# Queueing VectorE's attention side work behind the minima, moving late stores to GpSimd, and loading a branch's gates earlier

## The chip, the cores and the metric

The kernel runs on one core of a Trainium2 chip. The metric is device time in microseconds, the median of several executions. One further execution was recorded by the hardware profiler, and all rows below come from it.

## The reference

One hybrid decoder layer over 1024 tokens of width 1024, in float32:

```
h    = RMSNorm_pre(x)
proj = h @ w_in -> z_ssm | xBC | dt | q | k | v | f | z_att | g_ssm | g_att
A    = Mamba-2 chunked scan of conv+silu(xBC), gated by silu(z_ssm), group norm
B    = causal attention, 16 heads of 64:
       softmax(q.k/8 + F[t] - F[s]) @ v * silu(z_att),  F = cumsum(log_sigmoid(f))
m    = sigmoid(g_ssm) * (A @ w_branch_ssm) + sigmoid(g_att) * (B @ w_branch_att)
out  = x + RMSNorm_post(m @ w_out)
```

A is the recurrence branch ("ssm"), B the attention branch.

## The kernel before, in words

**Products in steps.** All large products run through a class `Stream`. It takes pairs of 128-column units and computes each 2 x 2 block product in seven steps (numbered 1 to 7) in place of eight, from sums of weight blocks and differences of data blocks. A step is 12 matmuls of 128 x 512; float32 operands are split into a high part (ScalarE copies into float32r) and a low part (VectorE subtracts). Split weights are called `wop` (L349, L350), split data operands `x0h`, `x0l` to `x6h`, `x6l` (L275 to L279). `Stream.half()` emits half a step. At a step's start it also calls `prepare`, which sums and splits the weights of the step three later, and `Operands.some`, which fetches and splits data operands of the next product that builds up. What a product is used for stands in handlers: `dst` gives the place of a result block, `post` works on it (tanh gates, silu gates, the gated branch results), and `begin` loads what `post` will need.

**The stages.** First normalisation and transposes; then the projections run beside the recurrence (generators `ssd` and `gate_and_norm`), one of four groups after another; then attention, with the remaining projections (the gates "za", "gs", "ga") and the product A @ w_branch_ssm ("wbs", handler `gated`) and the start of B @ w_branch_att ("wba") as filling between its parts; then the rest of "wba" and the product with w_out.

**Attention.** 8 pairs of heads with 6 visits each, 48 visits `m`. A visit does, in program order: `scores` (two query blocks for two heads, four score tiles `s`; VectorE adds the bias and takes the row minimum in one operation, L1471; ScalarE takes the exponential, L1475), the weighted sums of the visit before (`av`), `free` (VectorE scales the sums, L1423), `deferred` work (differences of attention outputs), `stream.release()`, some halves of the stream ("ahead"), `turned` (transposes `pt` of the exponentials, copied to SBUF as `p`, by VectorE at L1512 in blocks with b % 4 == 1 of the first six pairs of heads and by ScalarE at L1514 elsewhere), `stream.hold()`, and more halves ("behind"). Between `hold` and `release` the calls of `Operands.some` are collected, and `release` makes them after the next visit's scores; `prepare` is called at once.

**What sets the order.** TensorE's instructions stay in program order (`keep_in_program_order`). On the other engines a scheduler orders instructions ahead of the run by simulated readiness and priority; `tc.high_priority()` raises some, `pin` keeps an instruction behind the one traced before it on its engine, and `tc.issue_after(x)` keeps what is traced inside it behind x on x's engine, in issue order only. Once built, each engine and each queue of DMA issues runs strictly in order. SyncE (SP) issues nearly all loads; stores go through SP, ScalarE's queue (ACT) and GpSimd's (POOL).

**Small tiles.** `small()` gives one of four rotating 128 x 512 tiles (tag "th"), shared by gates, loads and results.

Of the kernel before, what the change touches and what calls it, by code (L numbers as in the profile page):

```python
# [23 lines left out]
NG = 4  # L24
# [62 lines left out]
def hybrid_layer(ctx: ExitStack, tc, a, out):  # L87

    nc = tc.nc
# [230 lines left out]
    class Pair:  # L320
# [95 lines left out]
                    nc.vector.tensor_tensor(d, s, ps, ALU.subtract)  # L416
            post(ch)

        def do(self, which):
            if which in (2, 4, 3) or which in (5, 7) and self.sums:  # L420
                unit, ch = {2: (0, 0), 4: (1, 0), 3: (0, 1)}.get(which, (1, 1))
                for begin in self.handlers[unit][2:]:
                    begin(ch)
            if which == 1:
                pool, tag = self.bank
                self.b = pool.tile([P, HALF], F32, tag=tag, bufs=1, name="pb")
                yield from self.matmuls(self.b, 1, "b11", True)
                self.k1 = self.keep(self.b)
            elif which == 2:
                pool, tag = self.other  # L430
                ps = pool.tile([P, HALF], F32, tag=tag, bufs=1, name="p" + tag)
                yield from self.matmuls(ps, 2, "b21", True)
                self.give(0, 0, ps, self.k1, "sum")
            elif which == 6:
                yield from self.matmuls(self.b, 6, "-t2", False)
                self.k2 = self.keep(self.b)
            elif which in (5, 7):
                if which == 5:
                    self.c = pj.tile([P, HALF], F32, tag="c", bufs=1, name="pc")
                    yield from self.matmuls(self.c, 5, "t1", True)  # L440
                else:
                    yield from self.matmuls(self.b, 7, "t3", False)
                    self.k7 = self.keep(self.b)
                self.sums += 1
                if self.sums == 2:
                    self.give(1, 1, self.c, self.k7, "less")
            elif which == 4:
                yield from self.matmuls(self.b, 4, "t4", False)
                self.give(1, 0, self.b)
            elif which == 3:  # L450
                yield from self.matmuls(self.c, 3, "-b22", False)
                self.give(0, 1, self.c, self.k2, "from")

    class Stream:
# [6 lines left out]
        def __init__(self, pairs, double, last):  # L461
            self.pairs = pairs
            for n, p in enumerate(pairs):
                p.bank, p.other = (pj, "be"[n % 2]), (pjx, "d") if n < double else (pj, "c")

                p.between = n < double or n >= last

            p, q, r = pairs[0:3]
            self.steps = [(p, 1), (q, 1), (p, 2), (q, 2)] + [(p, n) for n in (6, 5, 7, 4, 3)]
            self.steps += [(q, 6), (q, 5), (q, 7), (r, 1), (q, 4), (q, 3)]  # L470
            for n in range(2, last):
                p, nxt = pairs[n], pairs[n + 1]
                self.steps += [(p, i) for i in ((2, 6, 5, 7) if n < double else (6, 2, 7, 5))] + [(nxt, 1)]
                self.steps += [(p, 4), (p, 3)] if n + 1 < last else [(p, 3), (p, 4)]

            a, b, c, d, e, f, g, h = pairs[last:]
            self.steps += [(a, 5), (a, 6), (a, 7), (b, 1), (a, 2), (a, 4), (a, 3)]
            for p, nxt in ((b, c), (c, d), (d, e)):
                self.steps += [(p, 2), (p, 6), (p, 5), (p, 7), (nxt, 1), (p, 4), (p, 3)]
            self.steps += [(f, 1), (e, 2), (e, 6), (e, 5), (e, 7), (f, 2), (e, 4), (e, 3)]  # L480
            self.steps += [(f, 6), (f, 5), (f, 7), (g, 1), (f, 4), (f, 3)]
            self.steps += [(g, 2), (g, 6), (g, 5), (g, 7), (h, 1), (g, 4), (g, 3)]
            self.steps += [(h, 6), (h, 5), (h, 7), (h, 2), (h, 3), (h, 4)]
            self.following = {p: n.ops for p, n in zip(pairs, pairs[1:]) if n.ops is not p.ops}
            self.building = []
            self.chores, self.line = [], []
            self.held = None
            self.count = 0
            self.at = 0
            self.run = None  # L490
            self.waiting = []
            self.loads = [(p, names) for p in pairs for names in (("a11", "a12"), ("a21", "a22"))]
            self.loaded = []
            self.load_next()
# [23 lines left out]
                self.prepare(p, which)  # L518

        def prepare(self, p, which):  # L520
            p.prepare(which)
            self.load_more()

        def after(self, halves, fn):

# [2 lines left out]
        def half(self):  # L528
            if self.run is None:
                if self.at == len(self.steps):  # L530
                    return False
                p, which = self.steps[self.at]
                if which == 7 and p.ops is ops_a and "merged" not in fin:
                    return False
                if p.ops is ops_a and not all(p.ops.ready(OPERAND[which].strip("-"), j) for j in range(KH)):
                    return False
                self.ahead(False)
                for ops in self.building:
                    ops.some(OPERAND[which])
                self.run = p.do(which)  # L540
                next(self.run)
            else:
                for _ in self.run:
                    pass
                self.run = None
                p, which = self.steps[self.at]
                if p in self.following:
                    ops = self.following[p]
                    if ops not in self.building:
                        self.building.append(ops)  # L550
                    ops.open(OPERAND[which])
                self.ahead(True)
                self.at += 1
            for ops in self.building:
                if self.held is None:
                    ops.some()
                else:
                    self.held.append(ops)
            for chores in (self.chores, self.line):
                if chores:  # L560
                    chore = chores.pop(0)
# [13 lines left out]

        def release(self):
            held, self.held = self.held or [], None
            for ops in held:
                ops.some()

        def do_chores(self):
            while self.chores:
# [24 lines left out]
                self.halves(n)  # L607


    def tanh_gate(dram, i):  # L610

        t = {}

        def dst(ch):
            t[ch] = small()
            return t[ch]

        def post(ch):
            nc.scalar.activation(t[ch], t[ch], AF.Tanh, scale=0.5)
            nc.scalar.dma_start(dram[i, :, half(ch)], t[ch])  # L620

        return dst, post

    def silu_gate(dram, i):

        t = {}

# [4 lines left out]
        def post(ch):  # L632
            th = small()
            nc.scalar.activation(th, t[ch], AF.Tanh, scale=0.5)
            nc.vector.scalar_tensor_tensor(th, th, 1.0, t[ch], ALU.add, ALU.mult)
            nc.sync.dma_start(dram[i, :, half(ch)], th)

        return dst, post

# [335 lines left out]
    def gate_and_norm(g):  # L975
# [23 lines left out]
        for ch in range(2):  # L999
            sl = half(ch)  # L1000
            for j in range(2):
# [3 lines left out]
                        xs[j][:, sl], xs[j][:, sl], ng[:, i : i + 1], r[ch], ALU.mult, ALU.mult  # L1005
                    )
                )
                nc.sync.dma_start(ys_dram[i, :, sl], xs[j][:, sl])
                yield 1

    def weights_work():
# [23 lines left out]
    order = [p for ps in by_group for p in ps]  # L1035

    order[0:4] = [both("gs", 0, lambda i: tanh_gate(gs_dram, i))] + [order[n] for n in (2, 1, 3, 0)]
    late = [both("za", g, lambda i: silu_gate(za_dram, i)) for g in range(4)]
    late += [both("gs", g, lambda i: tanh_gate(gs_dram, i)) for g in range(1, 4)]
    late += [both("ga", g, lambda i: tanh_gate(ga_dram, i)) for g in range(4)]  # L1040


    fin = {}

    def gated(i):

        t = {}

        def begin(ch):
            t[ch] = small(), small()  # L1050
            nc.sync.dma_start(t[ch][1], gs_dram[i, :, half(ch)])

        def dst(ch):
            return t[ch][0]

        def post(ch):
            stream.after(1, lambda: times(*t[ch], ch))

        def times(y, g, ch):
            nc.vector.scalar_tensor_tensor(y, g, 1.0, y, ALU.add, ALU.mult)  # L1060
# [232 lines left out]
    with tc.tile_pool(name="att", bufs=1, reuse_waits="tile", side="right") as ap, tc.tile_pool(  # L1293
# [148 lines left out]
        def scores(hp, g, u):  # L1442
# [23 lines left out]
            for e in range(2):  # L1466
                o = ex[:, e, u, 0:w]
                nm = hd.at(hd.nm, i, h, e)
                with tc.high_priority():
                    pin(  # L1470
                        nc.vector.tensor_tensor_reduce(  # L1471
                            o, s[e][:, 0:w], fb[hp, h][:, e, 0:w], 1.0, 3.0e38, ALU.add, ALU.min, nm
                        )
                    )
                    pin(nc.scalar.activation(o, o, AF.Exp, scale=-1.0, bias=nm, accum_out=hd.at(hd.sm, i, h, e)))  # L1475

        def turned(hp, g, sent):

# [16 lines left out]
            for b in order:  # L1495
# [13 lines left out]
                with tc.high_priority():  # L1509

                    if b % 4 == 1 and hp < NK - 2:
                        nc.vector.tensor_copy(to, src)  # L1512
                    else:
                        nc.scalar.activation(to, src, AF.Copy)  # L1514
                made[b] = (hp, g, b, first, p)
# [135 lines left out]
        for m in range(6 * NK + 1):  # L1651
# [6 lines left out]
                    scores(hp, g, u)  # L1658
            for one in made:
                weighted(*one)  # L1660
            for hd, which in end(m - 1):
                hd.free(which)
            if m == 6 * NK:
                stream.release()
                heads[NK - 1].out(2)
                break
            for hd, which in end(m - 2):
                if hd.last and which and m < 6 * NK - 1:
                    hd.out(which)
            for fn in deferred:  # L1670
                fn()
            deferred.clear()
            stream.release()
            for hd, which in end(m):
# [84 lines left out]
```

## Time and profile before

| | us |
|---|---|
| median of 3 runs | 1279.64 |
| lowest, highest | 1279.46, 1281.26 |
| profiled execution | 1278.67 |
| its span, first to last instruction | 1277.0 |

The granted clock of TensorE was 0.998 of full speed. Attention's first scores start at 684.5 us and its last minima are past 1113 us. The profile gives, for each engine, busy time and the idle time before instructions with what ended it; PEld is TensorE's weight load, whose starts show when TensorE really began a matmul, since a matmul's end is modelled.

### The profile page before, as it was taken

The numbers are of one execution on the slowest core, as the hardware profiler recorded it, in microseconds if no ns is written. First come the engines' busy times: TensorE is split into PE (matmuls) and PEld (weight loads), VectorE is DVE, ScalarE is ACT, GpSimd is POOL, SyncE is SP. The second block draws the span as 40 slices with busy tenths as digits, with TensorE's granted clock in tenths as the row PEclk, the third lists the DMA queues.
The fourth block names the chain that finished last, engine by engine and source line by source line (L and its number), as shares of the span: only waits on it lengthen the run. The fifth ranks groups of instructions, "written<-read, shape, count | busy, mean of one in ns | idle before, by whom it ended". The sixth has DMA issues, their size and how long they took to land.

```text
span 1277.0 us, 20793 instructions
## 1 busy us (share of the span) xinstructions
PE 1246.0 (98%) x6926; PEld 980.9 (77%) x6926; DVE 1009.9 (79%) x1994; ACT 795.1 (62%) x1738; POOL 312.4 (24%) x314
## 2 busy tenths in 40 slices
PE   5999999999999999999999999999999999999997
PEld 3688888788788888888877777777767777778886
DVE  7988896888888978997766667767789767886975
ACT  7745665556665765566555666666677666744754
POOL 4000440013400241114102123313111212366052
PEclk9999999999999999999999999999999999999999
DMA  8233452546336533644447566666687657766932
GB/s 296 71 120 75 144 168 87 186 149 191 122 113 214 174 125 115 220 152 133 141 153 255 166 225 203 213 222 215 233 291 261 216 173 251 252 214 199 362 112 102
DMA packets 152747, 233.56 MB, mean 183 GB/s; under 512 B 15200, under 2 KB 60736, under 8 KB 152640
## 3 DMA queue, kind: packets, MB, share of 16 engines
q1 hardware_dynamic: 136640, 197.13, 47.4%
q10 hardware_dynamic: 11136, 19.11, 4.0%
q0 software_dynamic: 4864, 15.99, 3.3%
q8 instruction: 54, 0.88, 0.3%
q14 instruction: 53, 0.43, 0.1%
HBM read 162.99 MB, written 72.34 MB: 184 GB/s over the span
## 4 chain that ended last, share of the span: by engine, by line
PE 75%; DVE 8%; DMA 6%; ACT 5%; issue 4%; POOL 1%; SPq 1%; DVEq 0%; ACTq 0%; POOLq 0%
PE pb L128 31%; PE pc L128 18%; PE pd L128 6%; PE av L128 4%; PE pt L131 4%; PE s L128 4%; PE yps L128 2%; DVE wop L350 1%; ACT ex L1475 1%; PE st L128 1%; DMA xt<-in_x 1%; DMA th<-ys_dram 1%; DVE ex L1471 1%; PE tr L131 1%; PE tr_v L131 1%
## 5 line engine op out<-in xcount | busy, mean ns | idle before, releaser
L349 ACT ACTIVATE wop<-sum 128x512 fp32r<-128x512 f32 x180 | 112.5, 626 | 109.7 <-DVE sum L355 52.9
L350 DVE TENSOR_TENSOR wop<-sum,wop 128x512 fp32r<-128x512 f32 x180 | 137.8, 767 | 52.0 <-ACT wop L349 51.0
L1475 ACT ACTIVATE ex<-ex,nm 128x512 f32<-128x512 f32 (+1 forms) x192 | 116.2, 606 | 74.0 <-DVE nm L1471 73.2
L402 ACT ACTIVATE s<-pb 128x512 f32<-128x512 f32 x144 | 85.3, 592 | 95.7 <-PE pb L128 94.4
L128 PE MATMUL pc<-x2h,wop 128*128 128x512 f32 x384 | 130.4, 398 | 0.6 <-DVE u L414 0.6
L128 PE MATMUL pb<-x5h,wop 128*128 128x512 f32 x384 | 130.1, 396 | 1.0 <-ACT s L402 0.9
L128 PE MATMUL pb<-x0h,wop 128*128 128x512 f32 x384 | 130.8, 397 | 0.0
L128 PE MATMUL pb<-x6h,wop 128*128 128x512 f32 x384 | 129.5, 395 | 1.3 <-ACT s L402 1.3
L128 PE MATMUL pc<-x3h,wop 128*128 128x512 f32 x384 | 129.7, 395 | 0.4 <-DVE ot L416 0.4
L128 PE MATMUL pb<-x4h,wop 128*128 128x512 f32 x384 | 129.2, 395 | 0.0
L350 DVE TENSOR_TENSOR wop<-raw,wop 128x512 fp32r<-128x512 f32 x144 | 103.8, 722 | 28.4 <-ACT wop L349 27.9
L1471 DVE CUSTOM_DVE_ANT_0 ex<-s,fb 128x512 f32<-128x512 f32 (+1 forms) x192 | 97.0, 551 | 20.5 <-PE s L128 15.4
L349 ACT ACTIVATE wop<-raw 128x512 fp32r<-128x512 f32 x144 | 89.7, 624 | 11.4 <-PE pd L128 6.3
L128 PE MATMUL pd<-x1h,wop 128*128 128x512 f32 x288 | 96.3, 394 | 0.0
L128 PEld LDWEIGHTS pb<-x5h,wop 128*128 128x128 f32 x384 | 72.1, 188 | 18.9 <-ACT s L402 2.2
L128 PEld LDWEIGHTS pb<-x6h,wop 128*128 128x128 f32 x384 | 72.1, 188 | 18.6 <-issue 2.1
L128 PEld LDWEIGHTS pc<-x2h,wop 128*128 128x128 f32 x384 | 72.1, 188 | 18.6 <-issue 2.4
L128 PEld LDWEIGHTS pb<-x0h,wop 128*128 128x128 f32 x384 | 72.1, 188 | 17.4 <-issue 2.9
L128 PEld LDWEIGHTS pc<-x3h,wop 128*128 128x128 f32 x384 | 72.1, 188 | 17.1 <-issue 1.5
L128 PEld LDWEIGHTS pb<-x4h,wop 128*128 128x128 f32 x384 | 72.1, 188 | 16.7 <-issue 1.9
L211 POOL TENSOR_TENSOR wd<-wd 128x256 f32<-128x256 f32 x32 | 31.8, 995 | 206.1 <-DMA wd<-in_wo 120.9
L131 PE MATMUL pt<-ident,ex 128*128 128x128 f32 x576 | 75.5, 273 | 3.6 <-DVE nm L1471 1.8
(311 smaller groups left out, 2986.6 us busy)
## 6 DMA issues: line engine op xcount, KB each, us to landing
raw<-in_wu SPq DMA_DIRECT2D x128, 256.0 KB, 4.6
csb<-cs_dram SPq DMA_DIRECT2D x32, 256.0 KB, 6.5
q<-q_dram SPq DMA_DIRECT2D x32, 256.0 KB, 4.2
k<-k_dram SPq DMA_DIRECT2D x16, 512.0 KB, 6.7
fb<-f_dram SPq DMA_DIRECT2D x16, 512.0 KB, 5.7
rb<-st_dram SPq DMA_DIRECT2D x48, 128.0 KB, 3.1
wd<-in_wo SPq DMA_DIRECT2D x40, 128.0 KB, 2.5
xt<-in_x SPq DMA_DIRECT2D x8, 512.0 KB, 6.7
```

Source lines behind the costliest of these rows:

```text
L128: return tc.keep_in_program_order(nc.tensor.matmul(*args, **kw))
L131: return tc.keep_in_program_order(nc.tensor.transpose(out_, in_, idn))
L211: pin(nc.gpsimd.tensor_tensor(t[out_], t[a_], t[b_], ALU.subtract))
L349: nc.scalar.activation(op[:, 0], src, AF.Copy)
L350: nc.vector.tensor_tensor(op[:, 1], src, op[:, 0], ALU.subtract)
L402: nc.scalar.activation(s, ps, AF.Copy)
L1471: nc.vector.tensor_tensor_reduce(o, s[e][:, 0:w], fb[hp, h][:, e, 0:w], 1.0, 3.0e38, ALU.add, ALU.min, nm)
L1475: pin(nc.scalar.activation(o, o, AF.Exp, scale=-1.0, bias=nm, accum_out=hd.at(hd.sm, i, h, e)))
```

## The change

Three parts.

1. *Queueing.* `Stream.front` holds the last minimum of the running visit, and after the transposes VectorE's copy, where there is one. `stream.behind()` is `tc.issue_after(front)`: weight preparation, operand splits, released work, `free` and the deferred differences are traced inside it, so that VectorE issues them behind that instruction. `prepare` is now collected between `hold` and `release` too.
2. *Stores.* The silu gates "za", the attention gates "ga" of units 6 and 7, and the recurrence's result ys of the last group are stored through GpSimd's queue, in place of SP's, ScalarE's and SP's.
3. *Gates.* In `gated`, the load of the gate from gs_dram is marked `early` and made at the start of the step before the one that needs it; the tile of the result is now taken when the result is written.

```diff
-        def do(self, which):
-            if which in (2, 4, 3) or which in (5, 7) and self.sums:
+        def begin(self, which, sums, early):
+            if which in (2, 4, 3) or which in (5, 7) and sums:
                 unit, ch = {2: (0, 0), 4: (1, 0), 3: (0, 1)}.get(which, (1, 1))
                 for begin in self.handlers[unit][2:]:
-                    begin(ch)
+                    if hasattr(begin, "early") == early:
+                        begin(ch)
+
+        def do(self, which):
+            self.begin(which, self.sums, False)
...
         def prepare(self, p, which):
-            p.prepare(which)
+            if self.held is not None:
+                self.held.append(lambda: self.prepare(p, which))
+                return
+            with self.behind():
+                p.prepare(which)
             self.load_more()
+
+        def behind(self):
+
+            return nullcontext() if self.front is None else tc.issue_after(self.front)
...
+                if self.at + 1 < len(self.steps):
+                    after, then = self.steps[self.at + 1]
+                    after.begin(then, after.sums + (after is p and which in (5, 7)), True)
                 self.run = p.do(which)
...
                 if self.held is None:
-                    ops.some()
+                    with self.behind():
+                        ops.some()
                 else:
-                    self.held.append(ops)
+                    self.held.append(ops.some)
...
             held, self.held = self.held or [], None
-            for ops in held:
-                ops.some()
+            for fn in held:
+                with self.behind():
+                    fn()
...
-    def tanh_gate(dram, i):
+    def tanh_gate(dram, i, queue=nc.scalar):
...
-            nc.scalar.dma_start(dram[i, :, half(ch)], t[ch])
+            queue.dma_start(dram[i, :, half(ch)], t[ch])
...
-    def silu_gate(dram, i):
+    def silu_gate(dram, i, queue=nc.sync):
...
-            nc.sync.dma_start(dram[i, :, half(ch)], th)
+            queue.dma_start(dram[i, :, half(ch)], th)
...
-                nc.sync.dma_start(ys_dram[i, :, sl], xs[j][:, sl])
+                queue = nc.sync if g < NG - 1 else nc.gpsimd
+                queue.dma_start(ys_dram[i, :, sl], xs[j][:, sl])
...
-    late = [both("za", g, lambda i: silu_gate(za_dram, i)) for g in range(4)]
+    late = [both("za", g, lambda i: silu_gate(za_dram, i, nc.gpsimd)) for g in range(4)]
...
-    late += [both("ga", g, lambda i: tanh_gate(ga_dram, i)) for g in range(4)]
+    late += [both("ga", g, lambda i: tanh_gate(ga_dram, i, nc.gpsimd if i >= 6 else nc.scalar)) for g in range(4)]
...
-        t = {}
+        y, g = {}, {}
 
         def begin(ch):
-            t[ch] = small(), small()
-            nc.sync.dma_start(t[ch][1], gs_dram[i, :, half(ch)])
+            g[ch] = small()
+            nc.sync.dma_start(g[ch], gs_dram[i, :, half(ch)])
+
+        begin.early = True
 
         def dst(ch):
-            return t[ch][0]
+            y[ch] = small()
+            return y[ch]
...
-                    pin(
+                    least = pin(
                         nc.vector.tensor_tensor_reduce(
...
+            stream.front = least.ins
...
                     if b % 4 == 1 and hp < NK - 2:
-                        nc.vector.tensor_copy(to, src)
+                        copy = nc.vector.tensor_copy(to, src)
+                        stream.front = copy.ins
...
-            for hd, which in end(m - 1):
-                hd.free(which)
+            with stream.behind():
+                for hd, which in end(m - 1):
+                    hd.free(which)
             if m == 6 * NK:
+                stream.front = None
                 stream.release()
...
-            for fn in deferred:
-                fn()
+            with stream.behind():
+                for fn in deferred:
+                    fn()
```

More of the change, by code (lines that the diff above doesn't have):

```diff
@@ L487, in __init__ @@
             self.held = None
+            self.front = None
             self.count = 0
@@ L1037, in hybrid_layer @@
     order[0:4] = [both("gs", 0, lambda i: tanh_gate(gs_dram, i))] + [order[n] for n in (2, 1, 3, 0)]
[L1038 removed]
+    late = [both("za", g, lambda i: silu_gate(za_dram, i, nc.gpsimd)) for g in range(4)]
     late += [both("gs", g, lambda i: tanh_gate(gs_dram, i)) for g in range(1, 4)]
[L1040 removed]
+    late += [both("ga", g, lambda i: tanh_gate(ga_dram, i, nc.gpsimd if i >= 6 else nc.scalar)) for g in range(4)]
     fin = {}
     def gated(i):
[L1047 removed]
+        y, g = {}, {}
         def begin(ch):
[L1050 to L1051 removed]
+            g[ch] = small()
+            nc.sync.dma_start(g[ch], gs_dram[i, :, half(ch)])
+        begin.early = True
         def dst(ch):
[L1054 removed]
+            y[ch] = small()
+            return y[ch]
         def post(ch):
[L1057 removed]
+            stream.after(1, lambda: times(y[ch], g[ch], ch))
         def times(y, g, ch):
```

## The prediction

> **What bounds the kernel now.** I read the page's first part, then busy time by stretches of the attention stage, then the waits of the weight loads, then the timeline at the places where they wait.
>
> ```profile
> span 1277.0 us, 20793 instructions
> PE 1246.0 (98%) x6926; PEld 980.9 (77%) x6926; DVE 1009.9 (79%) x1994; ACT 795.1 (62%) x1738; POOL 312.4 (24%) x314
> ```
>
> ```profile
> 700.00:900.00 200.00, 199.86 (x1365) 152.62 (x1364) 138.66 (x376) 131.39 (x336) 54.43 (x68) 1.00 0.63 210
> 930.00:980.00 50.00, 46.78 (x313) 34.52 (x309) 44.69 (x112) 39.59 (x98) 7.80 (x12) 1.00 0.82 280
> 1080.00:1135.00 55.00, 53.89 (x319) 40.34 (x318) 48.96 (x106) 39.77 (x94) 22.64 (x21) 1.00 0.65 222
> 1130.00:1200.00 70.00, 69.91 (x309) 57.53 (x308) 55.06 (x72) 30.26 (x54) 36.51 (x25) 1.00 0.73 245
> ```
>
> The columns are length, then busy time of TensorE, its weight loads, VectorE, ScalarE and GpSimd, clock and DMA. TensorE is full nearly everywhere at full clock, so only its holes can be won. From 700 to 900 it lacks 0.14 us; from 930 to 980, where VectorE is busy 44.69 of 50 us, it lacks 3.2. Behind attention (1130 to 1200) it is full again, so a hole closed earlier carries to the end one to one. A matmul's modelled end hides part of a hole, so I price holes by the idle time of the weight loads:
>
> ```profile
> PEld s L128 <- ACT p L1514: 7.3, 21, 0.6
> PEld pt L131 <- ACT ex L1475: 3.2, 6, 1.1
> PEld pt L131 <- DVE nm L1471: 3.0, 5, 1.1
> PEld s L128 <- DVE p L1512: 2.7, 5, 1.4
> PEld s L128 <- DVE wop L350: 1.4, 4, 0.4
> ```
>
> These are the waits between 650 and 1135 us: total, times, longest. The 7.3 us in 21 pieces of 0.35 recur whenever the stream of projections hands over to the scores, whoever is named; I take them as the price of the hand-over, which the change leaves. Left are the transposes of a visit's exponentials, which wait for ScalarE's exponential or VectorE's minimum (6.2 us together), and one wait for VectorE's copy. No projection matmul (pb, pc) waits for a split weight (wop): the 1.4 is again the hand-over to the scores.
>
> Where the holes lie:
>
> ```profile
> 952.59 0.20 PEld L131 LDWEIGHTS pt<-ident,ex 128*128 128x128 f32 x2 [0.82 <-ACT ex L1475]
> 953.89 0.14 PEld L131 LDWEIGHTS pt<-ident,ex 128*128 128x128 f32 x1 [1.10 <-DVE nm L1471]
> 956.23 0.53 PEld L131 LDWEIGHTS pt<-ident,ex 128*128 128x128 f32 x5 [1.11 <-ACT ex L1475]
> 979.29 0.54 PEld L128 LDWEIGHTS s<-k,q 64*128 64x128 f32 x5 [1.37 <-DVE p L1512]
> 1076.35 0.14 PEld L131 LDWEIGHTS pt<-ident,ex 128*128 128x128 f32 x1 [0.84 <-DVE nm L1471]
> 1076.96 0.64 PEld L131 LDWEIGHTS pt<-ident,ex 128*128 128x128 f32 x6 [0.47 <-DVE nm L1471]
> 661.82 0.19 PEld L128 LDWEIGHTS pc<-x2h,wop 128*128 128x128 f32 x1 [0.47 <-DVE th L414]
> 668.01 0.19 PEld L128 LDWEIGHTS pc<-x1h,wop 128*128 128x128 f32 x1 [0.86 <-issue]
> ```
>
> Four places: 3.03 us at 952 to 956, 1.37 at 979, 1.31 at 1076, and 1.33 ahead of attention. With the rest of the 6.2 us (6.2 - 3.03 - 1.31, about 1.9) that is some 8.9 us, the ceiling of what the change can win.
>
> **The late stores to GpSimd.** The hole at 952 starts on ScalarE:
>
> ```profile
> 945.27 0.58 ACT L1514 ACTIVATE p<-pt 128x512 f32<-128x512 f32 x1
> 948.26 0.33 ACTq L620 DMA_DIRECT2D ga_dram<-th  x1
> 948.64 1.15 ACT L278 ACTIVATE x1h<-x1l 128x512 fp32r<-128x512 f32 x2 [2.79 <-DMA fb<-f_dram]
> ```
>
> ```profile
> 949.30 1.29 DVE L279 TENSOR_TENSOR x1l<-x1l,x1h 128x512 fp32r<-128x512 f32 x2 [1.22 <-ACT x1h L278]
> 950.85 0.68 DVE L1471 CUSTOM_DVE_ANT_0 ex<-s,fb 128x512 f32<-128x512 f32 x1
> ```
>
> ScalarE ends a copy at 945.85 and then sits before its store of an attention gate until 948.26; the wait ends with the landing of another transfer (fb), not with anything the store reads. Behind it stands x1h, behind that VectorE's x1l, and behind that the visit's first minimum at 950.85. This store is one of the last pair's four (i = 6, 7), which the change sends through GpSimd's queue. There the same wait, if it comes, holds only GpSimd. I take 3.0 of the 3.03 us. [...]
>
> What the move costs on GpSimd:
>
> ```profile
> L1061 POOL DMA_DIRECT2D ms_dram<-th x16 | 8.7, 547 | 67.9 <-DVE th L1060 46.7 <-DVE ns L1388 8.7 <-DVE sm L1385 6.6
> ```
>
> 16 silu stores, 4 gate stores and the last group's 4 ys stores are 24 x 0.55 = 13 us on an engine that is 24% busy. Each now waits at GpSimd's head for its VectorE result, and the mask additions behind it feed a minimum. I take nothing, with one store's 0.55 us in front of a mask as the upper bound.
>
> The ys and silu stores leave SP's queue, where they held back loads:
>
> ```profile
> 658.60 5.50 SPq L1008 DMA_DIRECT2D ys_dram<-xs  x3
> 679.66 5.06 SPq L636 DMA_DIRECT2D za_dram<-th  x2
> ```
>
> Fourteen half steps of projections stand ahead of the first score in TensorE's order, so earlier q, k and fb loads do not start attention sooner. What can shrink is the 1.33 us at 661 and 668, where VectorE runs late after waiting for loads. Bounds 0 and 1.33; I take 0.6, the middle, since no row says which load ended it.
>
> **The queueing on VectorE.** `front` is the visit's last minimum and, where VectorE copies, then the copy. Weight preparation, operand splits, `free` and the deferred differences may not be issued ahead of it, and preparation during the second half of a visit is put off until the next visit's scores. Today such work sits between minima:
>
> ```profile
> 931.58 0.69 DVE L276 SCALAR_TENSOR_TENSOR x4l<-x4l,x4h 128x512 fp32r<-128x512 f32 x1
> 932.28 0.66 DVE L1471 CUSTOM_DVE_ANT_0 ex<-s,fb 128x512 f32<-128x512 f32 x1
> ```
>
> ```profile
> ACT ex L1475 <- DVE nm L1471: 73.2, 58, 3.2
> ```
>
> Each inserted split delays all later exponentials of the visit by 0.69 us. The 73.2 us that ScalarE waits is mostly hidden, because projections run between scores and transposes; what reaches TensorE is the 1.9 us outside the named places. Work traced in the previous visit may still slip in, so I take a third, 0.6 (bounds 0 and 1.9). At 979 the copy is the last of a VectorE run:
>
> ```profile
> 976.42 0.69 DVE L350 TENSOR_TENSOR wop<-raw,wop 128x512 fp32r<-128x512 f32 x1
> 978.82 0.41 DVE L1512 COPY p<-pt 128x256 f32<-128x256 f32 x1
> ```
>
> If that split was prepared in the visit's second half, it goes behind the copy: 0.69 of 1.37 us. I take 0.7; the x2l splits around it were traced earlier and stay.
>
> What is late next? A split put off by about half a visit:
>
> ```profile
> 979.16 0.68 DVE L1471 CUSTOM_DVE_ANT_0 ex<-s,fb 128x512 f32<-128x512 f32 x1
> ...
> 942.73 1.29 DVE L276 SCALAR_TENSOR_TENSOR x4l<-x4l,x4h 128x512 fp32r<-128x512 f32 x2
> 963.22 0.39 PE L128 MATMUL pb<-x4h,wop 128*128 128x512 f32 x1
> ```
>
> This first minimum comes three visits after that of 950.85, so a visit takes 9.4 us and half of one 5. The last x4l ends at 944.0 and its first matmul starts at 963.2, so 19 us cover that 5. I price it at nothing; with the cover gone each visit's first split would hold TensorE for up to those 5 us.
>
> **The gates of the recurrence branch.** The load of gs moves to the start of the step before, 12 matmuls and what attention puts between them sooner, and ahead of the fetches that follow.
>
> ```profile
> 1064.75 0.81 SPq L263 DMA_DIRECT2D x0l<-ya_dram  x2
> 1066.14 0.38 SPq L1051 DMA_DIRECT2D th<-gs_dram  x1
> ```
>
> ```profile
> 1071.97 0.69 DVE L1060 SCALAR_TENSOR_TENSOR th<-th 128x512 f32<-128x512 f32 x1 [4.87 <-DMA th<-gs_dram]
> ```
>
> The load stood behind an operand fetch that SP could issue only at 1064.75, and VectorE stood 4.87 us with the next visit's minima behind it: that is the hole at 1076. A load one step sooner lands before it is wanted. I take 1.3 of 1.31. Its cost: the load takes a slot of the four shared 256 KB tiles earlier, and SP waits for the slot with q, k and v behind it.
>
> **Sum.** Won: 3.0 + 0.6 + 0.6 + 0.7 + 1.3 = 6.2 us. Against it I set 1.9 us for one new chance wait of the kind at 948 (3.0 us when it strikes; with every queue reordered I count it at about two thirds). That is an estimate from one event, with bounds 0 and two events, 6.0. Net -4.3. The profiled execution took 1278.67 us (span 1277.0 and 1.67 around it), and the median of the runs, 1279.64, lies 0.97 above: 1279.64 - 4.3 = 1275.3. If everything goes and nothing comes: 1270.7.
>
> **Rivals.** A measurement of this kernel can tell about 0.2%, 2.6 us, from no change.
>
> [...]
>
> *VectorE runs out of room (slower).*
>
> ```profile
> DVE ex L1471 <- PE s L128: 15.4, 18, 1.8
> ```
>
> Today VectorE fills the time before the scores and waits for them 18 times, 0.86 us each, in 48 visits. Queued strictly, it may wait in all of them. From 930 to 980 there are five visits and 5.3 us of room: from 1.06 us more idle per visit on, VectorE sets the pace. At the longest wait seen, 1.8 us, the stretch needs 44.69 + 9.0 = 53.7 us, and 1080 to 1135 (six visits, 48.96 + 10.8) needs 59.8: 3.7 + 4.8 = 8.5 us lost. Set against the gains outside these stretches (0.6 + 0.6 + 1.3 = 2.5), that is +6.0: 1285.6. For it: 89% busy in both. Against: operands there have 19 us of slack, so a backlog can spill into the next stretch.
>
> **Chances.** Forecast 0.60, the wait that moves 0.22, VectorE out of room 0.14, and 0.04 for a slot wait on SP that costs as much. From the same cases: faster 0.60, same 0.22, slower 0.18. The range goes from 1271.0 (nearly the ceiling) to 1281.8, which holds the second case and the mild part of the third; its far part, near 1285.6, is left out.
>
> **What would show it.** Right: the 952 hole gone and no ScalarE wait of over 2 us before x1h; the four minima of a visit without splits between them and ScalarE's 73.2 us clearly lower; VectorE's wait for gs (4.87) gone; the 979 hole at about 0.7. Wrong: new waits of pb or pc for wop or an x operand; VectorE's waits for the scores growing beyond 15.4 us by over 1 us a visit from 930 to 980; SP waiting before gs with q or k behind it; or TensorE as full as forecast and the time unchanged, which would say that the holes were not the price.

## The result, and the profile after

The changed kernel takes 1283.06 us (median of 22 runs) where the kernel before took 1279.42 on the same chip (22 runs). The medians lie 3.6 us apart; the ratio of the two kernels, which leaves out one run of each that took over 2000 us, is 1.0021, with a 95% interval of 1.0012 to 1.0030. That is slower by about 2.7 us, where the forecast was 1275.3 us, faster by 4.3. The profiled execution took 1283.68 us, with a span of 1282.0 against 1277.0. Ratios below are given in the same way, and a thousandth is 1.3 us.

The page's first part, of after:

```profile
span 1282.0 us, 20839 instructions
PE 1251.5 (98%) x6926; PEld 987.2 (77%) x6926; DVE 1015.7 (79%) x1994; ACT 795.3 (62%) x1738; POOL 327.5 (26%) x338
```

TensorE loads the same weights in the same order as before. Of the 5.0 us by which the profiled span is longer, 1.7 had come up by 600 us, as far as which every engine's order is that of before (VectorE's first 876 instructions are the same, one after the other, in both traces): that much differs between single executions (in the profiles of all the kernels below it lies between -1.9 and +1.7), and is not counted below. What the change did lies between 700 and 1135 us. The busy time by stretches of after (columns as in the prediction, the clock third from the right):

```profile
700.00:900.00 200.00, 199.38 (x1357) 151.90 (x1356) 140.04 (x379) 129.34 (x331) 57.07 (x68) 1.00 0.62 204
930.00:980.00 50.00, 48.80 (x322) 36.87 (x320) 46.48 (x114) 41.95 (x102) 10.02 (x14) 1.00 0.91 303
...
1080.00:1135.00 55.00, 52.45 (x307) 39.04 (x308) 49.26 (x109) 41.76 (x99) 15.90 (x18) 0.97 0.67 226
```

From 930 to 980 TensorE now lacks 1.2 us in place of 3.2: the hole at 952 is gone. But from 700 to 900, where 0.14 us was lacking, it lacks 0.62, and the end of attention is worse (2.55 us lacking in place of 1.11, with the mean clock down to 0.97). The holes themselves, in the timeline of after's weight loads (in brackets the idle time ahead of the row and what ended it):

```profile
721.29 0.47 PEld L128 LDWEIGHTS s<-k,q 64*128 64x128 f32 x6 [0.68 <-DVE p L1535]
...
797.50 0.18 PEld L128 LDWEIGHTS s<-k,q 64*128 64x128 f32 x1 [0.57 <-ACT p L1538]
...
877.25 1.16 PEld L128 LDWEIGHTS s<-k,q 64*128 64x128 f32 x11 [0.54 <-DVE p L1535]
...
980.65 0.53 PEld L128 LDWEIGHTS s<-k,q 64*128 64x128 f32 x5 [2.14 <-DVE p L1535]
...
1078.78 0.64 PEld L131 LDWEIGHTS pt<-ident,ex 128*128 128x128 f32 x6 [0.46 <-DVE nm L1493]
1079.90 0.74 PEld L131 LDWEIGHTS pt<-ident,ex 128*128 128x128 f32 x7 [0.49 <-ACT ex L1497]
1083.83 0.18 PEld L128 LDWEIGHTS s<-k,q 64*128 64x128 f32 x1 [0.62 <-ACT p L1538]
...
1113.55 0.18 PEld L128 LDWEIGHTS s<-k,q 64*128 64x128 f32 x1 [1.43 <-ACT p L1538]
```

The waits have changed their kind. Before, the longest were those of the transposes `pt` for minima and exponentials; now they are those of the scores `s` of the next visit for the copies `p` of this one, by VectorE (721, 877 and 980) or by ScalarE (797, 1083 and 1113). The minima did get what the change is built for, and the groups of the page and of the busy time by line show who pays (after):

```profile
L1497 ACT ACTIVATE ex<-ex,nm 128x512 f32<-128x512 f32 (+1 forms) x192 | 115.9, 605 | 59.0 <-DVE nm L1493 58.9
L1493 DVE CUSTOM_DVE_ANT_0 ex<-s,fb 128x512 f32<-128x512 f32 (+1 forms) x192 | 95.6, 553 | 38.1 <-PE s L128 31.6
L1535 DVE COPY p<-pt 128x512 f32<-128x512 f32 (+1 forms) x36 | 21.5, 598 | 18.9 <-PE pt L131 13.0 <-ACT st L1419 6.0
```

and the last of these groups in the kernel before:

```profile
L1512 DVE COPY p<-pt 128x512 f32<-128x512 f32 (+1 forms) x36 | 21.5, 597 | 8.3 <-PE pt L131 7.6 <-ACT st L1397 0.6
```

ScalarE waits 58.9 us for minima in place of 73.2. But VectorE stands 31.6 us waiting for scores in place of 15.4, and 13.0 us waiting for transposes in place of 7.6, each time with the queued work behind it. It has as much to do as before, and in all it stands no longer than before: from 700 to 1135 us it is busy 327.6 us in place of 327.2, and from 650 to 1135 its waits for ScalarE's half of a split weight fall from 31.2 to 15.5 us. So the waits have moved to places ahead of minima and copies, and work has moved from there into the stretch between a visit's last minimum and its copy. The visit before 980 shows this (VectorE's timeline of after, from the last minimum to the copy):

```profile
972.76 0.28 DVE L1493 CUSTOM_DVE_ANT_0 ex<-s,fb 128x128 f32<-128x128 f32 x1
972.97 0.08 DVE L1493 DVE_READ_ACCUMULATOR2_ANT nm<- 128x1 f32 x1
972.97 0.69 DVE L350 TENSOR_TENSOR wop<-raw,wop 128x512 fp32r<-128x512 f32 x1
973.57 1.28 DVE L276 SCALAR_TENSOR_TENSOR x2l<-x2l,x2h 128x512 fp32r<-128x512 f32 x2
974.78 0.68 DVE L1445 TENSOR_TENSOR o<-av,zr 128x512 f32<-128x512 f32 x1
975.38 0.68 DVE L1599 TENSOR_TENSOR x<-x,zr 128x512 f32<-128x512 f32 x1
975.98 0.68 DVE L279 TENSOR_TENSOR x6l<-x6l,x6h 128x512 fp32r<-128x512 f32 x1
976.58 0.68 DVE L412 TENSOR_TENSOR th<-pc,s 128x512 f32<-128x512 f32 x1
977.18 0.68 DVE L279 TENSOR_TENSOR x6l<-x6l,x6h 128x512 fp32r<-128x512 f32 x1
977.78 0.68 DVE L350 TENSOR_TENSOR wop<-raw,wop 128x512 fp32r<-128x512 f32 x1
978.38 1.28 DVE L276 SCALAR_TENSOR_TENSOR x2l<-x2l,x2h 128x512 fp32r<-128x512 f32 x2
979.59 0.68 DVE L1082 SCALAR_TENSOR_TENSOR th<-th 128x512 f32<-128x512 f32 x1
980.19 0.41 DVE L1535 COPY p<-pt 128x256 f32<-128x256 f32 x1
```

Twelve operations of 0.60 us stand one behind the other ahead of a copy at 980.19 whose transposes TensorE had ended by 976.5. In the kernel before, one of the two `wop` splits stood ahead of that visit's minima:

```profile
969.92 0.68 DVE L350 TENSOR_TENSOR wop<-raw,wop 128x512 fp32r<-128x512 f32 x1
970.53 0.41 DVE L1471 CUSTOM_DVE_ANT_0 ex<-s,fb 128x256 f32<-128x256 f32 x1
```

Over the 36 visits in which VectorE copies, the operations of 128 x 512 between last minimum and copy rise from 104 to 144 in the two traces, and the mean time from the one to the other from 3.95 to 4.37 us.

### The profile page after: what moved, and what is told of

Its sections match the earlier page's. It is cut to its first block, busy times and chain, and to the rows that moved or that the text cites. A ratio compares the mean times of both kernels' runs of the same rounds, so it can differ in the third digit from the quotient of the medians.

```text
span 1282.0 us, 20839 instructions
## 1 busy us (share of the span) xinstructions
PE 1251.5 (98%) x6926; PEld 987.2 (77%) x6926; DVE 1015.7 (79%) x1994; ACT 795.3 (62%) x1738; POOL 327.5 (26%) x338
## 4 chain that ended last, share of the span: by engine, by line
PE 74%; DVE 10%; DMA 7%; ACT 4%; issue 4%; POOL 1%; SPq 1%; DVEq 0%; ACTq 0%; POOLq 0%
PE pb L128 31%; PE pc L128 18%; PE pd L128 5%; PE av L128 5%; PE s L128 4%; PE pt L131 4%; PE yps L128 2%; DVE wop L350 2%; DVE sum L355 1%; DVE ex L1493 1%; DMA xt<-in_x 1%; ACT wop L349 1%; DMA raw<-in_wu 1%; PE tr_v L131 1%; PE st L128 1%
## 5 line engine op out<-in xcount | busy, mean ns | idle before, releaser
L1497 ACT ACTIVATE ex<-ex,nm 128x512 f32<-128x512 f32 (+1 forms) x192 | 115.9, 605 | 59.0 <-DVE nm L1493 58.9
L1493 DVE CUSTOM_DVE_ANT_0 ex<-s,fb 128x512 f32<-128x512 f32 (+1 forms) x192 | 95.6, 553 | 38.1 <-PE s L128 31.6
L888 POOL TENSOR_TENSOR xe<-xdt,tend 128x256 f32<-128x256 f32 x28 | 26.1, 930 | 196.7 <-DVE xdt L856 188.7
```

Source lines behind the costliest of these rows:

```text
L888: nc.gpsimd.tensor_tensor(xe, s["xdt"], tend[:, c, hs].unsqueeze(2).to_broadcast([P, 4, 64]), ALU.mult)
L1493: nc.vector.tensor_tensor_reduce(o, s[e][:, 0:w], fb[hp, h][:, e, 0:w], 1.0, 3.0e38, ALU.add, ALU.min, nm)
```

## The experiments

Sixteen kernels were run, each in five rounds beside the kernel before. The changed kernel is taken apart along these edits:

```diff
 Q  (all queueing)     = P and B below
 P  (the put-off)      -            if self.held is not None:
                       -                self.held.append(lambda: self.prepare(p, which))
                       -                return
 B  (issue behind)     -            return nullcontext() if self.front is None else tc.issue_after(self.front)
                       +            return nullcontext()
 S  (stores)           -  silu_gate(za_dram, i, nc.gpsimd)
                       +  silu_gate(za_dram, i)
                       -  tanh_gate(ga_dram, i, nc.gpsimd if i >= 6 else nc.scalar)
                       +  tanh_gate(ga_dram, i)
                       -  queue = nc.sync if g < NG - 1 else nc.gpsimd
                       +  queue = nc.sync
 G  (gates)            -  begin.early = True
                          (and y[ch] is taken in begin() again, beside g[ch])
```

**The parts alone.** `queue_only` undoes S and G, `stores_only` undoes Q and G, `gates_only` undoes Q and S; `queue_at_once` undoes S, G and P.

> The queueing alone; stores and gates as before. Theory 1 (VectorE's side work, pushed together behind the minima, stands as one run ahead of the next copy and minima): about +3 us, 1282.5, with a copy that comes over 1.4 us late near 980. Theory 2 (the early gates take tiles of the four that rotate, and others wait for a slot): this kernel keeps the gates as before, so no loss, 1277 to 1279.5. Theory 3 (GpSimd's stores hold masks): no loss either. ScalarE's wait for the minima (73.2 us) should fall to about 59, as in the changed kernel, in all of them.

> The moved stores alone. Theories 1 and 2: the hole at 952 goes (3.0 us) and nothing comes for it, 1276.5. Theory 3: VectorE's minima wait for masks that stand behind stores on GpSimd, 1281 or more, with VectorE's wait for the fb mask above the 4.8 us of before.

> The early gate loads alone. Theory 1: VectorE's 4.87 us wait for gs and the hole at 1076 go, 1278. Theory 2: waits for slots of the small tiles appear on SP, ScalarE or VectorE, and TensorE has a hole of over 1 us near 1113, 1281 to 1282.

> The queueing alone, but weight preparation in a visit's second half is made at once, as before, and not after the next scores. If the loss of theory 1 comes from putting preparation off, this is 1.5 us or more faster than the queueing alone; if it comes from the order behind the minima, both take the same time within 1 us. Theories 2 and 3: both as before.

Measured ratios to the kernel before: queueing alone 0.9993 (0.9980 to 1.0006), stores alone 1.0001 (0.9990 to 1.0013), gates alone 0.9986 (0.9972 to 1.0000), queueing without the put-off 0.9988 (0.9977 to 0.9999). No part loses by itself, so none of the three theories holds as it was put: the loss needs parts together. The put-off costs nothing that these runs can tell as long as the queueing is alone (0.9993 with it, 0.9988 without).

**The parts in pairs, and the whole again.** `queue_stores` undoes G, `queue_gates` undoes S, `stores_gates` undoes Q; `all_again` is the whole change.

> No part alone loses (queueing -0.9, stores 0, gates -1.8 us), all three lose 2.7 us. Theory A: the loss is the pair queueing and stores: the wait at 952 is gone, so work comes closer together and VectorE's run in front of the copy near 980 grows; this kernel shows a hole of about 2 us there, and where the granted clock falls to half behind it, 1.7 us more: 1281 to 1283. Theory B: the loss is the pair queueing and gates (slots of the small tiles near 1113): this kernel shows no hole over 1.2 us near 1113 and takes 1276 to 1279. [...]

> Theory A: no loss, 1277 to 1279, hole at 980 of 1.4 us or less. Theory B: the hole near 1113 of 1.4 us, ScalarE's copies held behind a small tile's slot, 1281 to 1283. [...]

> The change without the queueing. Theories A and B: no loss, the gains of stores and gates add up, 1276.5 to 1278.5. [...]

> The whole change once more, beside its pairs on one chip. Theories A and B: 2.7 us above the kernel before, within 1.3. [...]

Measured: queueing with stores 1.0008 (0.9997 to 1.0019), queueing with gates 0.9996 (0.9987 to 1.0006), stores with gates 0.9977 (0.9965 to 0.9988), the whole again 1.0016 (1.0004 to 1.0028). The loss is real, and it is the queueing added to the other two: from 0.9977 to 1.0016 or 1.0021, some 5 us. Theory A, the pair of queueing and stores, has the hole at 980 right: it is 2.18 us long with that pair, and 1.22 and 1.26 with queueing alone and with queueing and gates. But the pair's 1.0008 is at most half of the loss. Theory B, the pair of queueing and gates, missed the time (1279.76 us for 1281 to 1283), though waits of the kind that it named are there (below).

The clock alone is not the cause. The profile of `all_again` is of its fastest execution (1279.90 us) and has full clock from 21 to 1274 us, and yet that trace loses 3.2 us on the kernel before's between 700 and 1140. Over all runs the mean granted clock is 0.9974 for both `all_again` and the kernel before on that chip, and 0.9982 for `stores_gates`, about 1 us of their 5.

Since TensorE loads the same weights in the same order in every kernel, the traces also show where the time goes. The table gives the us by which the weight loads of a stretch (by the clock of before) take longer than before's; single traces of one kernel differ by about 1 us here, and the two figures with a star hold 1.7 us of half clock each (last section).

| stretch | changed kernel | `all_again` | `stores_gates` | `stores_gates_2` |
|---|---|---|---|---|
| 700 to 900 | +1.5 | +1.7 | -1.0 | +0.1 |
| 900 to 1000 | -0.4* | -0.8 | -0.5 | -0.4 |
| 1000 to 1090 | +0.4 | +0.9 | -1.9 | -1.4 |
| 1090 to 1140 | +2.0* | +1.4 | -0.2 | -0.1 |

So the queueing's price is not paid at 980, where what is gained at 952 outweighs it. It is paid in the small holes from 700 to 900 and, for the larger part, behind 1000.

The timeline of the weight loads of `stores_gates` shows what the other two parts are worth without the queue:

```profile
954.74 0.53 PEld L131 LDWEIGHTS pt<-ident,ex 128*128 128x128 f32 x5 [1.18 <-ACT ex L1494]
...
978.29 0.52 PEld L128 LDWEIGHTS s<-k,q 64*128 64x128 f32 x5 [0.82 <-DVE p L1532]
```

At 952 to 956, 1.18 us stands in one piece where 3.03 stood in three, and the hole at 979 shrinks from 1.37 to 0.82 without any queueing (0.72 with the stores alone); with it, it grows to 2.14 and more.

**Which piece of the queueing.** `all_at_once` undoes P alone, `putoff_no_queue` undoes B alone. `copy_front_only` lets work pass the minima and queues it behind the copy alone; `copy_on_scalar` gives VectorE's 36 copies to ScalarE:

```diff
 copy_front_only   -            stream.front = least.ins
 copy_on_scalar    -                    if b % 4 == 1 and hp < NK - 2:
                   -                        copy = nc.vector.tensor_copy(to, src)
                   -                        stream.front = copy.ins
                   -                    else:
                   -                        nc.scalar.activation(to, src, AF.Copy)
                   +                    nc.scalar.activation(to, src, AF.Copy)
```

> Stores and gates without the queueing win (1276.8), with it they lose (1282). Between a visit's last minimum and VectorE's copy stand, in issue order over all 36 such visits, 105 operations of 512 columns without the queueing and 144 with it. Theory A: these hold the copy, and TensorE's next scores wait for the score tile that the copy frees. Theory D: not the queue but the put-off preparation costs. This kernel is the whole change with preparation made at once: 117 such operations. Theory A: 1278 to 1279.5. Theory D: 1276.5 to 1277.5.

> Stores, gates and the put-off preparation, without any queueing: 99 operations between minimum and copy. Theory A: as without the queueing, 1276 to 1278. Theory D: 1280 or more.

> The whole change, put-off preparation too, but the front is the copy alone and never the minimum: 80 operations between minimum and copy. Theory A: no loss, 1275 to 1277.5, and the holes of 0.5 us or more that name the copy (717, 873, 978) are gone or under 1 us. Theory D: 1280 or more.

> The whole change with VectorE's 36 copies made by ScalarE, so that no copy stands behind VectorE's side work; ScalarE gets 36 times some 0.6 us, 21 us over 48 visits. Theory A: the holes that name VectorE's copy are gone, 1277 to 1280, less if ScalarE's copies come late in turn. Theory D: 1281 or more, as ScalarE only gets more to do.

Measured: without the put-off 0.9989 (0.9976 to 1.0001); the put-off without the queue 1.0047 (1.0035 to 1.0059, from five runs); queued behind the copy alone 0.9997 (0.9985 to 1.0009); copies on ScalarE 1.0000 (0.9988 to 1.0012). With stores and gates in the kernel the put-off is what loses: with the queue it costs 2.7 to 3.2 thousandths (0.9989 against 1.0016 and 1.0021, some 4 us), without it 7. What queueing without the put-off costs beside `stores_gates` (0.9989 against 0.9977) is inside the intervals. Either cure of the copy, its lead over all queued work or its move to ScalarE, brings the whole change back to no change, not to the 0.998 of `stores_gates`: operations ahead of the copy are part of the price, not all of it, and the time that theory A gave was met by `all_at_once` alone (theory D's by the other three). The traces say which part. In `copy_on_scalar` no hole of 0.45 us or more is left from 700 to 900, and in `copy_front_only` none either. Behind 1011 us no kernel has a copy on VectorE, so what is lost there is not lost ahead of a copy of its. Nor do 144 operations cost alike everywhere: `queue_only` and `queue_gates` have as many and take 0.9993 and 0.9996, and `queue_stores` has VectorE's, ScalarE's and GpSimd's whole order of the changed kernel at 1.0008. In `copy_front_only` only 80 operations of 128 x 512 stand between minima and copies in the order written out, fewer than before's 104, and what it loses it loses at the end of attention, where holes of 1.67, 0.74 and 2.34 us stand between 1105 and 1120.

**How the put-off alone can cost that much.** In the trace of `putoff_no_queue`, VectorE stands in front of a sum, with the visit's copy (773.96) behind it (first its timeline, then that of SP's queue):

```profile
772.99 0.69 DVE L355 TENSOR_TENSOR sum<-raw 128x512 f32<-128x512 f32 x1 [3.87 <-DMA raw<-in_wu]
```

```profile
766.27 1.09 SPq L1426 DMA_DIRECT2D rb<-st_dram  x2
767.40 1.05 SPq L342 DMA_DIRECT2D raw<-in_wu  x2
```

and SP's queue in the kernel before:

```profile
756.34 0.99 SPq L342 DMA_DIRECT2D raw<-in_wu  x2
...
766.64 1.09 SPq L1404 DMA_DIRECT2D rb<-st_dram  x2
```

`prepare` ends with `load_more`, which loads the raw weights of a later step. Put off with it, that load falls behind the `rb` loads of the stored statistics, which SP issues at 766.27: 767.40 in place of 756.34. VectorE's sum waits 3.87 us for it, the copy behind the sum is late, TensorE's scores wait 3.98 us for the copy, and the clock falls behind that (the stretches 774 to 778 and 778 to 785, clock 0.54 and 0.78):

```profile
774.00:778.00 4.00, 3.31 (x19) 2.48 (x21) 3.60 (x10) 0.81 (x2) 0.00 (x0) 0.54 0.23 86
778.00:785.00 7.00, 7.00 (x38) 4.72 (x35) 2.48 (x7) 2.71 (x8) 4.51 (x6) 0.78 0.18 60
```

Two runs test this by altering SP's order alone; every other engine's order stays as it was. `rb` is loaded after the put-off weights:

```diff
             for hd, which in end(m if m == 6 * NK - 1 else m - 1):
-                hd.take(which)
+                if hd.last:
+                    hd.take(which)
+                else:
+                    taken.append((hd, which))
...
             stream.release()
+            for hd, which in taken:
+                hd.take(which)
+            taken.clear()
```

> Stores, gates and the put-off, nothing queued behind a minimum or a copy, as in the run that was 0.47% slower; the one difference is on SP: each pair of rb loads is put after the put-off preparation's weight loads instead of ahead of them. Every other engine's order is the same. Theory S (the put-off moves the weight loads behind the rb loads, which wait for the statistics to be stored, and VectorE then stands for raw weights ahead of its copy): the 3.98 us hole at 774 with its 6.8 us at half clock goes, and the ratio falls from 1.0047 to 0.998 to 1.001. Theory V (what is put off costs on VectorE itself): the order on VectorE is unchanged, so the ratio stays at 1.003 to 1.006.

> The whole change, with only SP's order altered in the same way: rb loads after the put-off weight loads. Theory S: if late weight loads are also what the whole change pays, the ratio falls to 0.998 to 1.000. Theory V: VectorE's order is the same 144 operations between minima and copies, so the holes at 721, 797, 877 and 980 stay and the ratio stays at 1.001 to 1.002.

`putoff_take_late`: 1.0010 (0.9997 to 1.0023) in place of 1.0047. In its trace the load is issued at 756.20, ahead of `rb` at 765.56, and of the hole this is left:

```profile
770.01 1.16 PEld L128 LDWEIGHTS s<-k,q 64*128 64x128 f32 x11 [0.45 <-DVE p L1535]
```

So without the queue the put-off loses about half of its price on SP (3.7 of 7.0 thousandths). What is left of the loss lies at the end of attention, where that trace has a hole of 3.04 us at 1107 ahead of the transposes and half clock with it. `take_late`, the whole change with the same edit: 1.0020 (1.0009 to 1.0031), unchanged, and its hole too:

```profile
979.82 0.77 PEld L128 LDWEIGHTS s<-k,q 64*128 64x128 f32 x5 [2.20 <-DVE p L1535]
```

With the queue the late weights hold up little (VectorE's sums wait 1.0 us for them in the whole change), so there the loads' place on SP is not the price. VectorE's order is, as far as the holes from 700 to 900 and at 980 go; for what is lost behind 1000 that is not shown.

**The gates' gain, and the best version again.** `gates_pair` takes the product's tile together with the early gate (`y[ch], g[ch] = small(), small()` in the early `begin`); `stores_gates_2` is `stores_gates` once more, on another chip.

> The whole change, but the tile for the product is taken together with the tile for the early gate, one step sooner; no engine's order differs, only which of the four shared tiles a product gets. Theory T (ScalarE's copy of the product near 1072 waits 2.9 us for a tile that the store of t_a still reads, which eats what the early gate won): with another tile that wait goes, the small holes at 1078 to 1084 (0.46, 0.50, 0.63) shrink by 1 to 1.5 us together, and the ratio by 0.001. Rival: the wait is due to something else or moves to another tile; holes and ratio (1.001 to 1.002) as before.

> Stores and gates without any of the queueing, a second time on another chip: 0.9977 was measured. If that was not chance, 0.997 to 0.999; every theory that blames the queueing expects this.

`gates_pair`: 1.0018 (1.0007 to 1.0029), as the whole change; ScalarE's wait was still there, put down to another load:

```profile
1074.81 0.60 ACT L410 ACTIVATE th<-pb 128x512 f32<-128x512 f32 x1 [4.26 <-DMA x0l<-ya_dram]
```

The traces tell more than that name. In seven profiles (`after`, `all_again`, `all_at_once`, `queue_gates`, `copy_on_scalar`, `take_late` and this one) this copy waits 3.5 to 4.3 us and starts 0.15 to 0.16 us behind the landing of one store, `t_a<-y` (here 1074.65), whose source `y` is one of the four small tiles. These are the kernels with early gates and with work queued behind the minima; in the other eleven the copy starts before that landing. That the product was given that very tile is a reading: the profile doesn't print which of the four it is.

`stores_gates_2`: 0.9982 (0.9972 to 0.9993). Stores and gates without the queueing beat the kernel before, twice, by 2.3 to 2.9 us.

## Why the prediction was wrong, point by point

- **The hole at 952 (3.0): right in the whole change, too large for the stores alone.** ScalarE's long wait ahead of the store is gone. Its timeline of after, and then GpSimd's, where the store now stands behind an 8.84 us wait that holds no one:

```profile
948.66 0.62 ACT L637 ACTIVATE th<-th 128x512 f32<-128x512 f32 x1
949.18 1.14 ACT L278 ACTIVATE x1h<-x1l 128x512 fp32r<-128x512 f32 x2
```

```profile
949.57 0.56 POOL L638 DMA_DIRECT2D ga_dram<-th  x1 [8.84 <-ACT th L637]
```

  But with the stores alone a hole of 1.18 us stays at that place, with 0.47 behind it, and the interval of that run (0.9990 to 1.0013) leaves at most 1.3 us for all the stores: as a gain of the stores the term was too large by 1.7 us or more, and the rest of the hole goes only with the other parts.
- **The 0.6 at 661 and 668: not won.** At the two places the profile of after shows 0.47 and 1.18 us (655.37 and 675.47), against 0.47 and 0.86 before.
- **The queueing's 0.6 and the 0.7 at 979: the steps that failed, with their sign.** The prediction said that the split prepared in the visit's second half would go behind the copy. It did not: it still stands at 977.78, ahead of the copy, and the split that stood ahead of the minima joined it at 972.97. Work that passes a minimum is made not later than the copy but before it, because `front` is the minimum until `turned` sets it to the copy. The hole went from 1.37 to between 2.14 and 2.2 us, and holes of 0.5 to 0.7 came at 721, 797 and 877, in a stretch that had one, of 0.56 at 770.
- **"What is late next: nothing": the step that failed most.** It asked only whether TensorE would wait for an operand, and took the slack of 19 us from one place. At the end of attention there was none even before: the weight loads wait 0.30 and 0.41 us for `x3l` at 1116. In the profile of after there is no such wait at that place, but in others there is (0.93 us at 1119 in `all_again`, 2.34 in `copy_front_only`). It did not ask what else the put-off call does (its `load_more` on SP, worth 3.7 thousandths when nothing else hides it), nor what else comes late when VectorE's work stands in another order (the copies, and behind them the scores). Put at nothing, the queueing costs some 5 us where stores and gates are in the kernel.
- **The gates' 1.3: right alone, lost in company.** With the gates alone the transposes run in one piece (TensorE, `gates_only`):

```profile
1073.71 1.91 PE L131 MATMUL pt<-ident,ex 128*128 128x128 f32 x16
```

  In the whole change VectorE waits at the same place, no longer for gs but for the product (VectorE, then ScalarE, of after):

```profile
1075.59 0.69 DVE L1082 SCALAR_TENSOR_TENSOR th<-th 128x512 f32<-128x512 f32 x1 [5.08 <-ACT th L410]
```

```profile
1074.96 0.60 ACT L410 ACTIVATE th<-pb 128x512 f32<-128x512 f32 x1 [3.53 <-DMA t_a<-y]
```

  0.46 and 0.49 us of the 1.31 stay, and with the new 0.62 at 1083 the gain is gone: from 1070 to 1090 the weight loads take 0.6 us longer than before's in after, and 1.6 less in `gates_only` and `stores_gates`.
- **GpSimd's stores at nothing: right.** VectorE's minima wait 4.0 us for masks, 4.8 before.
- **The chance wait (1.9): a size met by luck.** The new hole of 1.43 us at 1113 is near it, but it is no chance: `all_again` has it too (1.35). ScalarE's `st` stands ahead of the copies there:

```profile
1112.97 0.27 ACT L1419 ACTIVATE st<-pt 8x128 f32<-8x128 f32 x1 [0.58 <-DMA ms_dram<-th]
```

  `st` is a small tile as well. It starts 0.08 or 0.09 us behind the landing of a store out of another (`ms_dram<-th`) in the six profiles of kernels that have the queueing behind the minima, the put-off and the gates together, after a wait of 0.56 to 1.33 us, and waits for no store in the others.
- **The rivals.** The wait that moves, 0.22 of the chances, did not come: from 943 to 952 ScalarE waits for no landing in after, and its longest wait there is 2.10 us, for VectorE. VectorE out of room came in its sign: the wait for scores grew by 16.2 us. But over 48 visits that is 0.34 each, under the 1.06 from which that rival decided, and not from 930 to 980, where it is 1.8 us in two waits. The slot wait on SP, at 0.04, is nearest to the waits at 1075 and 1113, but it came on ScalarE and not on SP. The loss from 700 to 900 came from the order of what VectorE does behind the minima, which no rival had. How the loss behind 1000 divides between the two waits on ScalarE and the rest stays open; no run took these waits away.

## What to carry to other kernels

Queued behind the minima, work stood ahead of the copies on the same engine (144 operations in place of 104): before queueing work behind A, list what comes next on that engine after A, and price the delay of that (here the copy, with three holes of 0.5 to 0.7 us and one that grew from 1.37 to 2.14). Of a call that is put off, list the loads that it issues and what they then stand behind in their queue. Where tiles rotate, look at the landing of the stores that read them (here, after waits of 3.5 to 4.3 us, a copy started 0.15 to 0.16 us behind one). Parts that are harmless alone can lose together, so measure the parts added to each other; here two of three were the better kernel.

## What the runs showed of the hardware

Some holes in TensorE's work cost more than their length here. After's holes of 2.14 us at 980 and 1.43 us at 1113 were each followed by 3.41 us at half clock (from 982.54 and from 1115.66), some 1.7 us lost each time. The stretch right behind the first, which takes in the edge of the slow one, shows a clock of 0.55:

```profile
982.20:985.60 3.40, 3.40 (x12) 2.60 (x9) 2.50 (x13) 2.07 (x7) 0.00 (x0) 0.55 0.84 288
```

In `all_again` a hole of 2.19 us at the same matmul was followed by full clock. The two slow stretches of after begin 133.1 us apart, 39 times 3.413 us. Four other profiles have two such stretches between 900 and 1140 us, and theirs lie 39, 39, 43 and 45 times that length apart (133.1, 133.1, 146.8 and 153.6 us). The length of a hole alone did not decide: the shortest hole with half clock right behind it was 1.10 us (`queue_at_once`, at 1109), and the longest without it 2.34 us (`copy_front_only`, at 1120).
